# A ring of five tiles instead of four for gathered expert rows, in a streaming-encoder layer on one Trainium2 core

## The chip, the core and the metric

The kernel runs on one core of one Trainium2 chip. The metric is device time in microseconds (us) of one execution. A core has a matrix engine (TensorE; PE in the profile, its weight loads PEld), a vector engine (VectorE, DVE), a scalar engine (ScalarE, ACT), a general engine (GpSimd, POOL) and a queue engine (SyncE, SP). Each engine runs its own instructions in the order in which they stand in the program, and waits on semaphores for the others. DMA transfers are issued from SP, ACT and, where the rows to be read are chosen by an index, from POOL.

## What is computed

One layer of an encoder is applied to 1024 prompt tokens and 8 x 16 sample tokens, 1152 rows of 1024 floats, which the kernel treats as nine tiles of 128 tokens. The parts are two kinds of attention, a merge, and then a product-key retrieval of single-neuron experts (PEER):

```
q = (xi @ w_q).reshape(t, PEER_HEADS, 2, PEER_DK // 2)
s = jnp.einsum('thpc,hpnc->thpn', q, sub_keys).astype(jnp.float32)
top_s, top_i = lax.top_k(s, PEER_TOPK)
...
idx = jnp.take_along_axis(cand_i, pos, axis=-1)
g = jax.nn.softmax(best_s, axis=-1)
hid = jax.nn.gelu(jnp.einsum('thkd,td->thk', u[idx], xi).astype(jnp.float32))
wgt = (g * hid).astype(xi.dtype)
return jnp.einsum('thk,thkd->td', wgt, v[idx])
```

Each token chooses 8 heads x 16 = 128 of 16384 experts. An expert has one row of `u` and one of `v`, of 1024 floats each. A last step adds a gated per-layer embedding (PLE).

## The kernel before

The nine tiles are two groups: group 0 is tiles 8, 0, 1, 2 and group 1 is tiles 3 to 7. Both go through a norm, the attention units (`project`, `prompt`, `decode`), the merge (`merge_phase`) and the routing (`route_phase`, which finds the top 16 with `topk16`, L733 to L737, and makes the expert indices, L744 to L802).

The experts are then done in two ways.

- **Group 0 gathers.** For each of its four tiles POOL issues 128 indirect DMAs, each of which brings one `u` row per token (128 x 1024 floats, 512 KB), and DVE forms the dot product with the token's row in one instruction (L821, with a small read of the accumulator behind it). After a GELU and the gate, 128 indirect DMAs bring the `v` rows, and DVE adds each, weighted, into `gya` (L823). These are 1024 gathers (L818) and 1024 DVE steps of 128 x 1024. They are the steps of a generator, `gather_steps`, and every gathered tile comes from one ring:

```
r = gat.tile([P, D], F32, tag="ring", name=f"{'uv'[k // P]}{t}_{k % P}", bufs=RING)
nc.gpsimd.indirect_dma_start(out=r, out_offset=None, in_=I["pu" if k < P else "pv"],
                             in_offset=bass.IndirectOffsetOnAxis(ap=gi[:, kk:kk + 1], axis=0))
```

- **Group 1 is dense.** `hidden` computes all 16384 hidden values of its 640 tokens in 128 blocks `j` (L969, `hd`), `expand_phase` turns the routing into a dense weight matrix (L923 to L940, kept in DRAM as `G_d`), and `dense_phase` multiplies and sums: per block `j` DVE multiplies hidden values with weights (L998, `ge`), ACT and DVE split `ge`, `us` and `vs` in a high and a low part (L951, L952), and PE sums the products in groups of four blocks (L1020 to L1022, `py`), which DVE adds to `yacc` (L1023). Of the 128 blocks 36 (`PRE`) have their hidden values computed ahead, during the routing, with GpSimd forming the low parts.

Where the gathers stand is set in two places. `gathers(G0)` hands out 400 steps when group 0's routing is done, at the lowest priority, so they are spread over group 1's attention, merge and routing. `dense_phase` hands out `G1` = `G2` = 5 steps per block `j`, not ahead of that block's split (`issue_after`), until all 1024 are used. The rest is the scheduler's: it plays the program through a timeline of its own and puts, on each engine, what is ready and of highest priority next. Four tiles of 4 KB per partition form the ring, so gather number k can start once the DVE step of gather k - 4 has ended. POOL issues the gathers in order, among its other work (memsets L333, powers L215, low parts L198 and L952, products L929).

By the trace the execution falls in five stages. I name them for later use:

- **A** (0 to 860 us): group 0's attention, merge and routing; no gathers.
- **B** (860 to 1620): group 1's attention and merge, with gathers.
- **C1** (1620 to 1963): group 1's routing on DVE, with the last of the 400 gathers, and the ahead-of-time hidden values on PE.
- **C2** (1963 to 2206): `expand_phase`.
- **D** (2206 to 3830): `dense_phase`, with 624 gathers. PLE (161 us) ends the program.

Of the kernel before, what the change touches and what calls it, by code (L numbers as in the profile page):

```python
# [31 lines left out]
SETUP = -1500  # L32
SC = 3
NH = (6, 5)
RING = 4
GD = 2
SR = 2
UNITS = (4, 0, 1, 5, 2, 6, 3, 7)
# [8 lines left out]
def build(tc, I, O, dbg=None, stop=None):  # L47
# [758 lines left out]
    def gather_steps(tiles, res):  # L806

        for t in tiles:
# [6 lines left out]
            for k in range(2 * P):  # L815
                r = gat.tile([P, D], F32, tag="ring", name=f"{'uv'[k // P]}{t}_{k % P}", bufs=RING)
                kk = k % P
# [384 lines left out]
```

## Time and profile before

| | |
|---|---|
| median of 3 runs | 3990.67 us (3986.85 to 3994.92) |
| the profiled execution, its own time | 3992.47 us |
| its span, first to last instruction | 3990.7 us |
| busy: PE, DVE, POOL, ACT | 3611.7, 2952.4, 1862.6, 1477.4 us |
| mean granted TensorE clock | 0.962 of full speed |
| moved by DMA | 1002.51 MB, 251 GB/s over the span; by the gathers 536.94 MB |

The profile gives, for each group of like instructions, its busy time and the idle time of its engine just ahead of it, with what ended that idle time. A busy share is an average over stages; a stage is read by its own window. The chain of work that ended last is followed back from the last instruction, at each step to what released it. Matmuls overlap in the records, so a group's busy time is a union and the mean length of one is more than its share.

### The profile page before, as it was taken

Reading aid. Unit: us, or ns where it says so; the run is one execution under the profiler, and the core shown is the slowest. Engines: PE = TensorE matmul, PEld = TensorE weight load, DVE = VectorE, ACT = ScalarE, POOL = GpSimd, SP = SyncE. Lnnn points to the kernel's source line nnn. Section 1 sums busy time; section 2 is a strip of 40 time slices with the busy share of each in tenths; the row PEclk is TensorE's granted clock in tenths of the full one; section 3 lists DMA queues with packets and bytes.
Section 4 is the critical chain, followed back from the end, with each engine's and each line's share of the span. In section 5 each row is a group of like instructions: output and inputs, shape, how many; then the busy total and the mean of one; then the engine's idle time right before and its main releaser. Section 6 shows DMA issues by size and latency. Waiting matters only on the chain.

```text
span 3990.7 us, 57379 instructions
## 1 busy us (share of the span) xinstructions
PE 3611.7 (91%) x20520; PEld 2990.8 (75%) x20520; DVE 2952.4 (74%) x5610; ACT 1477.4 (37%) x3379; POOL 1862.6 (47%) x1436
## 2 busy tenths in 40 slices
PE   7999898768888897899887999999999999999989
PEld 6656566656665565888887888888888888888866
DVE  5222113999878777899888688887889888888862
ACT  6555413356666311324578322222222222222231
POOL 5112122157676555663465355555555555555510
PEclk9999999889999998999999999999999999999999
DMA  7888625148888888983254898998999988989842
GB/s 218 251 261 244 191 64 193 48 134 258 285 277 273 303 303 304 328 263 114 99 216 211 290 317 303 320 320 294 320 312 316 326 313 300 320 310 322 303 152 70
DMA packets 415118, 1002.51 MB, mean 251 GB/s; under 512 B 38816, under 2 KB 170352, under 8 KB 412400
## 3 DMA queue, kind: packets, MB, share of 16 engines
q0 software_dynamic: 147456, 536.94, 39.1%
q1 hardware_dynamic: 237568, 397.63, 30.4%
q10 hardware_dynamic: 29808, 64.28, 4.2%
q8 instruction: 162, 2.65, 0.3%
q14 instruction: 124, 1.02, 0.1%
HBM read 917.19 MB, written 81.50 MB: 250 GB/s over the span
## 4 chain that ended last, share of the span: by engine, by line
PE 25%; DVE 22%; issue 20%; DMA 19%; POOL 12%; ACT 1%; POOLq 0%; SPq 0%; ACTq 0%; DVEq 0%
DMA v<-in_pv,gi 9%; POOL u L818 6%; DMA u<-in_pu,gi 5%; POOL v L818 4%; DVE u L821 4%; DVE gya L823 3%; PE hd L969 2%; PE pg L938 2%; PE Sd L552 2%; POOL ga L929 2%; PE pu L643 1%; DMA vs<-in_pv 1%; PE z L207 1%; PE z L208 1%; PE py L1020 1%
## 5 line engine op out<-in xcount | busy, mean ns | idle before, releaser
L818 POOL DMA_INDIRECT v<-in_pv,gi x512 | 669.6, 1308 | 595.5 <-DVE gya L823 466.9
L818 POOL DMA_INDIRECT u<-in_pu,gi x512 | 675.8, 1320 | 499.1 <-DVE u L821 361.0
L821 DVE SCALAR_TENSOR_TENSOR u<-u,gn 128x1024 f32<-128x1024 f32 x512 | 642.2, 1262 | 175.1 <-DMA u<-in_pu,gi 172.1
L823 DVE SCALAR_TENSOR_TENSOR gya<-v,hid,gya 128x1024 f32<-128x1024 f32 x512 | 661.3, 1292 | 116.6 <-DMA v<-in_pv,gi 112.3
L1020 PE MATMUL py<-vh,wh 128*128 128x512 f32 x1280 | 509.6, 400 | 61.8 <-DVE yacc L1023 35.5
L1021 PE MATMUL py<-vl,wh 128*128 128x512 f32 x1280 | 503.2, 394 | 0.3 <-DVE vl L952 0.3
L1022 PE MATMUL py<-vh,wl 128*128 128x512 f32 x1280 | 498.6, 394 | 3.3 <-DVE wl L952 3.3
L969 PE MATMUL hd<-aTh,ul 128*128 128x320 f32 x2048 | 483.8, 314 | 12.5 <-POOL ul L952 10.5
L969 PE MATMUL hd<-aTh,uh 128*128 128x320 f32 x2048 | 486.1, 315 | 7.8 <-ACT gp L972 4.9
L969 PE MATMUL hd<-aTl,uh 128*128 128x320 f32 x2048 | 483.2, 313 | 0.0
L969 PEld LDWEIGHTS hd<-aTh,ul 128*128 128x128 f32 x2048 | 350.5, 191 | 20.3 <-POOL ul L952 13.5
L969 PEld LDWEIGHTS hd<-aTh,uh 128*128 128x128 f32 x2048 | 352.7, 191 | 15.9 <-ACT gp L972 5.7
L969 PEld LDWEIGHTS hd<-aTl,uh 128*128 128x128 f32 x2048 | 351.5, 191 | 4.7
L1020 PEld LDWEIGHTS py<-vh,wh 128*128 128x128 f32 x1280 | 243.4, 190 | 122.4 <-DVE yacc L1023 43.8
L951 ACT CAST vh<-vs 128x1024 fp32r<-128x1024 f32 x128 | 133.9, 1052 | 461.6 <-PE py L1022 235.1
L1022 PEld LDWEIGHTS py<-vh,wl 128*128 128x128 f32 x1280 | 243.5, 190 | 56.0 <-DVE wl L952 5.3
L1021 PEld LDWEIGHTS py<-vl,wh 128*128 128x128 f32 x1280 | 243.9, 191 | 47.7 <-DVE vl L952 0.6
L951 ACT CAST wh<-ge 128x640 fp32r<-128x640 f32 x128 | 91.8, 727 | 436.6 <-PE py L1021 233.3
L951 ACT CAST uh<-us 128x1024 fp32r<-128x1024 f32 x128 | 134.3, 1049 | 276.0 <-PE hd L969 253.9
L1023 DVE TENSOR_TENSOR yacc<-yacc,py 128x1024 f32<-128x1024 f32 x160 | 192.5, 1215 | 16.0 <-PE py L1022 14.2
L938 PE MATMUL pg<-obb,ga 128*128 128x128 f32 x1280 | 163.8, 281 | 36.0 <-POOL ga L929 15.9
L938 PEld LDWEIGHTS pg<-obb,ga 128*128 128x128 f32 x1280 | 153.0, 191 | 45.6 <-POOL ga L929 20.0
(1053 smaller groups left out, 7260.4 us busy)
## 6 DMA issues: line engine op xcount, KB each, us to landing
us<-in_uT SPq DMA_DIRECT2D x128, 512.0 KB
vs<-in_pv SPq DMA_DIRECT2D x128, 512.0 KB
G_d<-stage ACTq DMA_DIRECT2D x10, 4096.0 KB
gj<-G_d SPq DMA_DIRECT2D x64, 640.0 KB
kcd<-in_kA SPq DMA_DIRECT2D x128, 256.0 KB
vcd<-in_vA SPq DMA_DIRECT2D x128, 256.0 KB
ge_d<-gp ACTq DMA_DIRECT2D x36, 320.0 KB
ge<-ge_d SPq DMA_DIRECT2D x36, 320.0 KB
```

What stands on the lines that cost most here:

```text
L552: nc.tensor.matmul(ps[32 * b4:32 * b4 + 32, :], q3[:, 4 * s + b4, :], rhs, start=br == 1 and q < nch, stop=True)
L818: nc.gpsimd.indirect_dma_start(out=r, out_offset=None, in_=I["pu" if k < P else "pv"], in_offset=bass.IndirectOffsetOnAxis(ap=gi[:, kk:kk ...
L821: nc.vector.scalar_tensor_tensor(r, r, 1.0, n2, op0=OP.mult, op1=OP.mult, accum_out=hid[:, kk:kk + 1])
L823: nc.vector.scalar_tensor_tensor(ya, r, hid[:, kk:kk + 1], ya, op0=OP.mult, op1=OP.add)
L929: nc.gpsimd.tensor_tensor(ga[:, c, :], oa[:, b, :, :].rearrange("p i c -> p c i"), gT[:, c0 + 4 * b:c0 + 4 * b + 4].unsqueeze(2).broadcast ...
L938: nc.tensor.matmul(pg[:, c * P:(c + 1) * P], ga[:, b0 + c, :], ob[:, b0 + c, :], start=True, stop=True)
L951: nc.scalar.copy(out_h, src)
L969: nc.tensor.matmul(ps[sp][:, 0:Nw], a[:, k, :], b[:, k, sp * Nw:(sp + 1) * Nw], start=k == 0 and q == 0, stop=k == 7 and q == 2)
L1020: nc.tensor.matmul(py[:, c], wh[:, ns], vh[:, c], start=a, stop=False)
L1021: nc.tensor.matmul(py[:, c], wh[:, ns], vl[:, c], start=False, stop=False)
L1022: nc.tensor.matmul(py[:, c], wl[:, ns], vh[:, c], start=False, stop=z)
L1023: nc.vector.tensor_tensor(yacc[n], yacc[n], py, op=OP.add)
```

## The change

One constant is changed. It is used once, as the number of buffers of the tag `ring` (L817).

```
-RING = 4
+RING = 5
```

The ring takes 4 KB more per partition, and gather k can start once the DVE step of gather k - 5 has ended. No instruction is added or taken out. Since the scheduler works with the ring's releases, the order on every engine changes from the first gathers on.

On VectorE in stage B, at the gathers of the first tile, this is before. `u` with a number is a gathered tile and `gn` the tokens' rows; the other rows are attention and the routing of a later tile (`oh`, `mn`, `kq`, `sm`).

```order
L821 SCALAR_TENSOR_TENSOR u_28_7958,hid_7873<-u_28_7958,gn_7869 128x1024
L450 RECIPROCAL sm_10175<-sm_10175 128x1
L794 TENSOR_TENSOR oh_7732<-oh_7732 128x64x8
L821 SCALAR_TENSOR_TENSOR u_29_7961,hid_7873<-u_29_7961,gn_7869 128x1024
L794 TENSOR_TENSOR oh_7724<-oh_7724 128x64x4
L317 TENSOR_TENSOR kq_10226<-kq_10226,kq115r 128x256
L821 SCALAR_TENSOR_TENSOR u_30_7964,hid_7873<-u_30_7964,gn_7869 128x1024
L794 TENSOR_TENSOR oh_7732<-oh_7732 128x64x4
L481 TENSOR_REDUCE mn_10280<-N_10274 128x1
L794 TENSOR_TENSOR oh_7724<-oh_7724 128x64x2
L318 TENSOR_TENSOR kq_10226<-kq_10226,kn 128x128
```

At the same place, with the same `oh` and the next `kq` and `mn`, the changed kernel has this.

```order
L821 SCALAR_TENSOR_TENSOR u_37_7985,hid_7873<-u_37_7985,gn_7869 128x1024
L794 TENSOR_TENSOR oh_7724<-oh_7724 128x64x4
L481 TENSOR_REDUCE mn_10367<-N_10361 128x1
L794 TENSOR_TENSOR oh_7732<-oh_7732 128x64x4
L450 RECIPROCAL sm_10283<-sm_10283 128x1
L821 SCALAR_TENSOR_TENSOR u_38_7988,hid_7873<-u_38_7988,gn_7869 128x1024
L821 SCALAR_TENSOR_TENSOR u_39_7991,hid_7873<-u_39_7991,gn_7869 128x1024
L317 TENSOR_TENSOR kq_10337<-kq_10337,kq116r 128x256
L794 TENSOR_TENSOR oh_7724<-oh_7724 128x64x2
L481 TENSOR_REDUCE mn_10392<-N_10386 128x1
```

Gather 37 now stands where gather 29 stood: the gathers stand more densely among the attention's steps. By the last norm step of the merge (L673) 339 gathers have been used before the change and 359 after it.

On VectorE at the head of C1, where the routing's top-16 search begins, the rows before the change are these. `tops`, `topi` and `sc` are the search's values, indices and scores, and `wq..l` a low part of the query weights.

```order
L821 SCALAR_TENSOR_TENSOR u_91_8923,hid_8649<-u_91_8923,gn_8645 128x1024
L733 MAX tops_14975<-sc_15046 128x8 x2
L733 MAX tops_14976<-sc_15060 128x8 x2
L734 MAX_INDEX topi_14980<-tops_14975,sc_15046 128x8 x2
L734 MAX_INDEX topi_14981<-tops_14976,sc_15060 128x8 x2
L735 MATCH_REPLACE sc_15046<-tops_14975,sc_15046 128x128 x2
```

And in the changed kernel the search begins behind another gather.

```order
L821 SCALAR_TENSOR_TENSOR u_112_8986,hid_8649<-u_112_8986,gn_8645 128x1024
L706 TENSOR_TENSOR wq12l<-wq12s,wq12h 128x1024
L733 MAX tops_14975<-sc_15046 128x8 x2
L733 MAX tops_14976<-sc_15060 128x8 x2
L734 MAX_INDEX topi_14980<-tops_14975,sc_15046 128x8 x2
L734 MAX_INDEX topi_14981<-tops_14976,sc_15060 128x8 x2
L735 MATCH_REPLACE sc_15046<-tops_14975,sc_15046 128x128 x2
```

The first steps of the search stand behind `u_112` instead of `u_91`, so of the 400 gathers 21 fewer follow the search's beginning.

In stage D the number of gathers by each group of four blocks stays nearly the same (417, 434, 451, 472 used after the first four groups before, 417, 435, 452, 471 after), and only their places between the dense steps move. On VectorE, in one group of D, before:

```order
L1023 TENSOR_TENSOR yacc_20596<-yacc_20596,py_23011 128x1024
L823 SCALAR_TENSOR_TENSOR gya_8647<-v_115_22498,hid_8649,gya_8647 128x1024
L1023 TENSOR_TENSOR yacc_20597<-yacc_20597,py_23037 128x1024
L823 SCALAR_TENSOR_TENSOR gya_8647<-v_116_22573,hid_8649,gya_8647 128x1024
L823 SCALAR_TENSOR_TENSOR gya_8647<-v_117_22576,hid_8649,gya_8647 128x1024
L823 SCALAR_TENSOR_TENSOR gya_8647<-v_118_22579,hid_8649,gya_8647 128x1024
L823 SCALAR_TENSOR_TENSOR gya_8647<-v_119_22582,hid_8649,gya_8647 128x1024
L823 SCALAR_TENSOR_TENSOR gya_8647<-v_120_22585,hid_8649,gya_8647 128x1024
L1023 TENSOR_TENSOR yacc_20598<-yacc_20598,py_23063 128x1024
```

The same stretch in the changed kernel:

```order
L1023 TENSOR_TENSOR yacc_20596<-yacc_20596,py_23011 128x1024
L823 SCALAR_TENSOR_TENSOR gya_8647<-v_117_22576,hid_8649,gya_8647 128x1024
L1023 TENSOR_TENSOR yacc_20597<-yacc_20597,py_23037 128x1024
L823 SCALAR_TENSOR_TENSOR gya_8647<-v_118_22579,hid_8649,gya_8647 128x1024
L823 SCALAR_TENSOR_TENSOR gya_8647<-v_119_22582,hid_8649,gya_8647 128x1024
L823 SCALAR_TENSOR_TENSOR gya_8647<-v_120_22585,hid_8649,gya_8647 128x1024
L823 SCALAR_TENSOR_TENSOR gya_8647<-v_121_22788,hid_8649,gya_8647 128x1024
L823 SCALAR_TENSOR_TENSOR gya_8647<-v_122_22791,hid_8649,gya_8647 128x1024
L1023 TENSOR_TENSOR yacc_20598<-yacc_20598,py_23063 128x1024
```

The gathers run two further ahead of `yacc` here, and as many stand between two additions as before. On SP, the loads and stores around a gathered tile (L811, L813, L828) move a few places forward among the weight loads, with the gathers that they belong to.

## The prediction

> **What bounds the kernel now.** I read the page's chain of waits first, then the table of stages, then the groups of instructions and the waits of each stage, and last the timeline of a few microseconds.
>
> ```profile
> ## 4 chain that ended last, share of the span: by engine, by line
> PE 25%; DVE 22%; issue 20%; DMA 19%; POOL 12%; ACT 1%; POOLq 0%; SPq 0%; ACTq 0%; DVEq 0%
> DMA v<-in_pv,gi 9%; POOL u L818 6%; DMA u<-in_pu,gi 5%; POOL v L818 4%; DVE u L821 4%; DVE gya L823 3%; PE hd L969 2%; PE pg L938 2%; PE Sd L552 2%; POOL ga L929 2%; PE pu L643 1%; DMA vs<-in_pv 1%; PE z L207 1%; PE z L208 1%; PE py L1020 1%
> ```
>
> The gathers, with POOL's issue, the transfer and the DVE step, are 31% of the chain (9 + 6 + 5 + 4 + 4 + 3), although PE is the busiest engine. The stages B, C1, C2, D and the PLE, in this order:
>
> ```profile
> core 0: us, PE busy (x) PEld busy (x) DVE busy (x) ACT busy (x) POOL busy (x), PEclk, DMA share, GB/s
> 860.00:1620.00 760.00, 648.00 (x3431) 475.81 (x3431) 620.74 (x1095) 357.89 (x939) 487.75 (x413) 0.94 0.86 287
> 1620.00:1963.00 343.00, 307.61 (x1924) 296.85 (x1925) 331.13 (x1300) 118.71 (x197) 168.74 (x99) 0.94 0.60 199
> 1963.00:2206.00 243.00, 207.05 (x1597) 197.37 (x1598) 206.63 (x242) 192.02 (x507) 142.52 (x84) 0.99 0.46 187
> 2206.00:3830.00 1624.00, 1555.77 (x8241) 1379.68 (x8239) 1376.65 (x1517) 377.05 (x535) 846.98 (x621) 0.99 0.89 311
> 3830.00:3991.00 161.00, 148.22 (x576) 106.48 (x576) 59.21 (x80) 37.27 (x60) 4.41 (x8) 0.95 0.28 93
> ```
>
> B has no full engine: PE is idle for 112 us and DVE for 139. C1 is DVE's (331 of 343 us). D is nearly PE's (1556 of 1624), with DVE and the DMA engines (0.89) close behind. What leaves DVE idle in B are these groups:
>
> ```profile
> L821 DVE SCALAR_TENSOR_TENSOR u<-u,gn 128x1024 f32<-128x1024 f32 x211 | 261.5, 1245 | 76.2 <-DMA u<-in_pu,gi 73.8 <-issue 1.7 <-DVE sm L450 0.3
> L823 DVE SCALAR_TENSOR_TENSOR gya<-v,hid,gya 128x1024 f32<-128x1024 f32 x128 | 164.0, 1281 | 44.9 <-DMA v<-in_pv,gi 44.1
> ```
>
> 118 of the 139 idle us are DVE standing at a gathered row that has not landed (73.8 + 44.1). In D the same groups, with what PE waits for there:
>
> ```profile
> L823 DVE SCALAR_TENSOR_TENSOR gya<-v,hid,gya 128x1024 f32<-128x1024 f32 x368 | 472.2, 1283 | 71.8 <-DMA v<-in_pv,gi 68.2
> L821 DVE SCALAR_TENSOR_TENSOR u<-u,gn 128x1024 f32<-128x1024 f32 x256 | 310.0, 1221 | 96.1 <-DMA u<-in_pu,gi 95.5
> DVE u L821 <- DMA u<-in_pu,gi: 95.5, 72, 4.4
> DVE gya L823 <- DMA v<-in_pv,gi: 68.2, 67, 3.4
> PE py L1020 <- DVE yacc L1023: 35.5, 27, 3.7
> PE py L1020 <- ACT wh L951: 20.9, 14, 3.8
> PE py L1020 <- ACT vh L951: 5.4, 2, 5.1
> ```
>
> DVE loses 164 us to gathers in D, in 139 waits of 1.2 us on average. PE loses about 62 us there, 35.5 of it directly to additions of DVE that come late, and 20.9 to `wh`, which ACT makes from DVE's `ge`.
>
> **How long a gather takes.** The ring's turn shows in D, in DVE's rows and one of POOL's:
>
> ```profile
> 3007.79 1.28 DVE L823 SCALAR_TENSOR_TENSOR gya<-v,hid,gya 128x1024 f32<-128x1024 f32 x1
> 3009.72 1.28 DVE L823 SCALAR_TENSOR_TENSOR gya<-v,hid,gya 128x1024 f32<-128x1024 f32 x1
> ...
> 3018.60 1.28 DVE L823 SCALAR_TENSOR_TENSOR gya<-v,hid,gya 128x1024 f32<-128x1024 f32 x1 [0.86 <-DMA v<-in_pv,gi]
> ...
> 3011.27 0.93 POOL L818 DMA_INDIRECT v<-in_pv,gi  x1 [0.66 <-DVE gya L823]
> ```
>
> The step at 3009.72 ends at 3011.00 and frees its tile; POOL starts the gather at 3011.27; the step that uses it starts at 3018.60, after a wait. So from release to use a gather needs 7.6 us here, and with four tiles only the three steps between and whatever the program puts among them cover it. With five tiles this gather would be released by the step at 3007.79, which ends 1.93 us earlier. That is more than its wait of 0.86.
>
> **The change part by part.** Nothing is added or taken out, so each term is stall that goes, or work that moves.
>
> *D: stalls.* Each gather gets at least one more DVE step as cover, 1.22 to 1.28 us by the rows above, and on average the 2.5 us between two gathers of D (1624 us / 624). The average wait is 1.2 us, the longest 4.4. So most of the 139 waits go; I keep a quarter, 40 of 164 us, since the scheduler also moves steps. The numbers of gathers per group of blocks stay, so no DVE work moves into D. The end gains only what PE gains. Its floor comes from two stretches without waits:
>
> ```profile
> 3107.07 0.39 PE L1020 MATMUL py<-vh,wh 128*128 128x512 f32 x1
> ...
> 3113.19 0.39 PE L1020 MATMUL py<-vh,wh 128*128 128x512 f32 x1
> 3179.70 0.46 PE L969 MATMUL hd<-aTh,ul 128*128 128x320 f32 x2
> ...
> 3182.34 0.46 PE L969 MATMUL hd<-aTh,ul 128*128 128x320 f32 x2
> ```
>
> 27 `py` matmuls in 6.12 us are 0.227 us each, and 18 `hd` in 2.64 are 0.147. By the code the stage has 128 blocks x 30 (five tiles, two halves, three products) = 3840 of the first, and (128 - 36) blocks x 48 = 4416 of the second: 871 + 648 = 1519 us. So D cannot fall by more than 105 us, and of this only the 62 of waits belong to DVE or ACT. I take 40 of the 62: all but a few of the `yacc` waits and a part of the `wh` waits. The bounds are 0 (the transfers, already at 0.89, give nothing) and 62.
>
> *B: stalls against denser work.* The waits behind the 118 us:
>
> ```profile
> DVE u L821 <- DMA u<-in_pu,gi: 73.8, 72, 5.3
> DVE gya L823 <- DMA v<-in_pv,gi: 44.1, 50, 2.6
> DVE kq L317 <- POOL kq135r L215: 1.4, 1, 1.4
> ```
>
> They would fall to about 40 by the same reasoning (122 waits of 0.97 us on average; one step more is at least 1.2, but the scheduler here packs the steps more densely, which takes part of the cover back). Against it, 20 more gathers stand in B: 20 x (1.25 + 0.08 for the read of the accumulator) = 27 us of DVE work, the 0.08 from this row:
>
> ```profile
> L821 DVE DVE_READ_ACCUMULATOR u<-u,gn 128x1 f32 x210 | 17.0, 81 | 0.0
> ```
>
> DVE's clock in B thus gains 78 - 27 = 51 us. PE has 112 idle us there, but part of these are waits on ACT that no gather causes:
>
> ```profile
> PE mt13t L224 <- DVE tg L647: 17.4, 2, 16.5
> PE po L503 <- ACT pT L80: 15.2, 12, 4.4
> PE pt L496 <- ACT pT L80: 14.4, 12, 3.1
> PE pt L496 <- ACT p L451: 9.5, 3, 5.8
> ```
>
> The first is DVE late at the merge's end and can go whole; the `pT` waits stay. I take 30 us, between 0 and 51. One reason excludes less than nothing unless transfers slow down: the added 27 us are smaller than the stall that the ring's turn must lose.
>
> *C1: work that leaves.* The routing's search stands behind fewer gathers, and DVE is its bound. The prices there:
>
> ```profile
> L821 DVE SCALAR_TENSOR_TENSOR u<-u,gn 128x1024 f32<-128x1024 f32 x46 | 72.0, 1571 | 2.8 <-DMA u<-in_pu,gi 2.8
> L823 DVE SCALAR_TENSOR_TENSOR gya<-v,hid,gya 128x1024 f32<-128x1024 f32 x16 | 25.1, 1568 | 0.0
> ```
>
> A step takes 1.57 us in C1 and 1.25 in B. In C1, POOL forms the low parts for the hidden values at the same time. 20 steps that leave are worth 20 x 1.57 = 31 us; at B's price they would be 25. I take 28. C2 starts when the routing is done, so it moves forward whole; its own length stays (243 us, PE, DVE and POOL in turn).
>
> The Trainium skill, "SBUF — State Buffer", section "Who interferes with whom", says that a VectorE instruction with two SBUF inputs and a GpSimd instruction that reads SBUF lock each other out of a shared port for a whole instruction. By that rule the longer step is such a lock, and the term would be the 31; without it the 25. The 1.571 against 1.245 agrees in direction.
>
> *At no cost:* the 4 KB of memory; the loads of `gn` and `gya` that move forward on SP, by a few weight loads, and stay prefetches; POOL's small work in B (memsets, powers), queued behind gathers that now wait less. If that cover failed, the nearest price is the last row above, 1.4 us of DVE behind a power in all of B.
>
> *The sum.* -30 (B) -28 (C1) -40 (D) = -98 us. The profiled execution took 3992.47 us (span 3990.7), 1.8 above the median of 3990.67. 3992.5 - 98 = 3894.5; set against the median it is 3893. I give 3894.
>
> **The rivals.**
>
> 1. *Transfers or PE take D over.* DVE's stalls shrink, but D is at 0.89 of the DMA engines and PE at 96%, so D gains 5 us or none, and only B and C1 count, somewhat cut: -58 to -63, about 3932. For it: D moves 311 GB/s over 1624 us, and the best of the page's 40 slices is 328:
>
> ```profile
> GB/s 218 251 261 244 191 64 193 48 134 258 285 277 273 303 303 304 328 263 114 99 216 211 290 317 303 320 320 294 320 312 316 326 313 300 320 310 322 303 152 70
> ```
>
> At that rate D could fall to 1624 x 311 / 328 = 1540 at best. Against it: that still leaves 84 us, more than the 40. Chance 0.24.
>
> 2. *The change does nothing that counts.* The scheduler plans with the same fifth tile, so it sets the steps so much closer that the cover stays as it was. The order in B goes this way (gather 37 where 29 stood), but in D the count per group is unchanged. 3990, chance 0.06.
>
> 3. *A fifth gather in flight makes each slower.* With five tiles the ring turns as fast as before if the time from release to use grows by 5/4, from 7.6 to 9.5 us. Beyond that it is a loss. The place is B and D, where 122 + 139 waits show the ring as the limit. At 10.1 us each such step would come (10.1 / 5) - (7.6 / 4) = 0.12 us later than now, 31 us if all 261 stay ring-bound; and the 27 us that B takes on are not paid back by its stalls, but C1 returns its 28. So about +30, 4022. For it: DMA share 0.86 and 0.89 in the two stages. Against it: gathers are the same number and bytes, and more in flight adds no traffic. Chance 0.10.
>
> The Trainium skill, "DMA: Bandwidth & Descriptors", section "Queues, rings and completion order", says that a DMA engine takes turns between queues by whole packets, and drains a queue's ring in order. By that rule a fifth gather stands behind the other four of its queue and lands no sooner where the queue is never empty, which is rival 1 or 3. The queue rows speak against a full queue: the gathers' own packets take 39.1% of the engines' span.
>
> ```profile
> q0 software_dynamic: 147456, 536.94, 39.1%
> q1 hardware_dynamic: 237568, 397.63, 30.4%
> ```
>
> **How the numbers follow.** The forecast has 0.60: 3894, with its own range from all terms high (62 + 51 + 31 = 144, 3848) to half of each (3943). With the rivals' 0.24, 0.06 and 0.10 the chances sum to one. The range that should hold 8 in 10 runs from 3850 to 3985: it leaves out rival 3, rival 2 and the very best case. What a measurement of this kernel can tell from no change is about 0.2%, 8 us. Faster by more: forecast and rival 1, 0.84. Same: 0.06. Slower: 0.10.
>
> **What would show it.** In the profile after: DVE's idle time at L821 and L823 behind DMA falls from 118 to about 40 us in B and from 164 to about 40 in D; `PE py <- DVE yacc` falls from 35.5 below 15; B is about 730 us long, C1 about 315, D about 1584. C2 keeps its 243. The forecast is wrong if D stays above 1615 while DVE's stalls go (rival 1), if the stalls stay near 280 us in all (rival 2), or if the time from a release to its use rises over 9.5 us (rival 3).

## The result, and the profile after

| | before | after |
|---|---|---|
| median | 3992.8 us (3986.85 to 3999.76, 4 runs) | 3864.45 us (3856.23 to 3871.44, 4 runs) |
| profiled execution | 3992.47 us | 3856.23 us |
| mean granted TensorE clock | 0.962 | 0.968 |

The ratio is 0.968, with a 95% interval of 0.966 to 0.969: 128 us less by the medians, 136 by the two profiled executions. The forecast was 3894, its range 3850 to 3985.

The chain of waits of the changed kernel (shares of the span, by engine and by line) is now PE's:

```profile
PE 50%; DVE 20%; issue 11%; DMA 9%; POOL 7%; ACT 3%; SPq 0%; ACTq 0%; POOLq 0%; DVEq 0%
PE hd L969 11%; PE py L1022 5%; PE py L1020 5%; PE py L1021 5%; POOL v L818 3%; PE pu L643 3%; DVE u L821 2%; POOL u L818 2%; DMA u<-in_pu,gi 2%; PE Sd L552 2%; DVE gya L823 2%; PE zg L208 2%; PE zg L209 2%; PE zg L207 2%; PE pg L938 2%
```

The gathers' lines, 31% of the chain before, are 11% here (3 + 2 + 2 + 2 + 2); the transfers of `v`, 9% before, have dropped out of the list. The dense matmuls stand at its head. The table of stages of the changed kernel has the columns of the one before: window, length, busy time of PE, PEld, DVE, ACT and POOL, granted clock, DMA share, GB/s.

```profile
core 0: us, PE busy (x) PEld busy (x) DVE busy (x) ACT busy (x) POOL busy (x), PEclk, DMA share, GB/s
867.00:1597.00 730.00, 640.87 (x3401) 472.57 (x3399) 635.27 (x1112) 354.98 (x923) 529.41 (x432) 0.95 0.90 314
1597.00:1914.00 317.00, 283.31 (x1784) 274.45 (x1785) 294.89 (x1258) 114.18 (x189) 132.03 (x74) 0.94 0.52 174
1914.00:2155.00 241.00, 216.28 (x1718) 210.09 (x1717) 222.94 (x242) 197.42 (x515) 152.39 (x87) 1.00 0.49 198
2155.00:3696.00 1541.00, 1530.90 (x8261) 1371.37 (x8259) 1372.84 (x1517) 377.39 (x537) 874.59 (x620) 1.00 0.93 327
3696.00:3855.00 159.00, 144.34 (x576) 104.20 (x576) 58.66 (x80) 37.29 (x60) 5.35 (x8) 0.98 0.28 94
```

Against the rows before, B is 760 to 730, C1 343 to 317, C2 243 to 241, D 1624 to 1541, the PLE 161 to 159. D fell most, by 83 us, twice what was forecast for it. PE is now busy for 1530.90 of D's 1541 us.

DVE's waits in D, and below them PE's, with total, times and longest in us:

```profile
DVE yacc L1023 <- PE py L1022: 37.1, 25, 4.8
DVE u L821 <- DMA u<-in_pu,gi: 32.7, 25, 2.8
...
DVE gya L823 <- DMA v<-in_pv,gi: 16.3, 22, 1.4
...
PE py L1020 <- ACT wh L951: 4.9, 5, 2.9
PE py L1022 <- DVE wl L952: 1.8, 3, 1.2
...
PE py L1020 <- DVE yacc L1023: 0.4, 1, 0.4
```

DVE's stalls behind gathered rows fell from 164 to 49 us (32.7 + 16.3), and `yacc <- PE` (14.2 before, 37.1 now) has taken the first place in DVE's list. PE hardly waits for DVE any more. In B the same groups read:

```profile
DVE u L821 <- DMA u<-in_pu,gi: 41.0, 56, 2.7
DVE gya L823 <- DMA v<-in_pv,gi: 11.8, 21, 1.6
...
PE mt13t L224 <- DVE tg L647: 5.3, 1, 5.3
```

118 became 53 us, and PE's wait at the merge's end 17.4 became 5.3.

### The profile page after: what moved, and what is told of

Its sections match the earlier page's. It is cut to its first block, busy times and chain, and to the rows that moved or that the text cites. A ratio compares the mean times of both kernels' runs of the same rounds, so it can differ in the third digit from the quotient of the medians.

```text
span 3854.5 us, 57390 instructions
## 1 busy us (share of the span) xinstructions
PE 3571.1 (93%) x20520; PEld 2973.5 (77%) x20520; DVE 2949.6 (77%) x5610; ACT 1480.2 (38%) x3379; POOL 1911.3 (50%) x1436
## 4 chain that ended last, share of the span: by engine, by line
PE 50%; DVE 20%; issue 11%; DMA 9%; POOL 7%; ACT 3%; SPq 0%; ACTq 0%; POOLq 0%; DVEq 0%
PE hd L969 11%; PE py L1022 5%; PE py L1020 5%; PE py L1021 5%; POOL v L818 3%; PE pu L643 3%; DVE u L821 2%; POOL u L818 2%; DMA u<-in_pu,gi 2%; PE Sd L552 2%; DVE gya L823 2%; PE zg L208 2%; PE zg L209 2%; PE zg L207 2%; PE pg L938 2%
## 5 line engine op out<-in xcount | busy, mean ns | idle before, releaser
L818 POOL DMA_INDIRECT v<-in_pv,gi x512 | 697.6, 1362 | 488.6 <-DVE gya L823 368.8
L818 POOL DMA_INDIRECT u<-in_pu,gi x512 | 689.7, 1347 | 398.4 <-DVE u L821 264.4
L821 DVE SCALAR_TENSOR_TENSOR u<-u,gn 128x1024 f32<-128x1024 f32 x512 | 620.4, 1228 | 80.7 <-DMA u<-in_pu,gi 76.6
L1020 PE MATMUL py<-vh,wh 128*128 128x512 f32 x1280 | 498.2, 391 | 7.1 <-ACT wh L951 4.9
L1023 DVE TENSOR_TENSOR yacc<-yacc,py 128x1024 f32<-128x1024 f32 x160 | 193.4, 1214 | 40.7 <-PE py L1022 37.1
L938 PE MATMUL pg<-obb,ga 128*128 128x128 f32 x1280 | 157.1, 277 | 24.7 <-POOL ga L929 10.5
L929 POOL TENSOR_TENSOR ga<-oa,gT 128x512 f32<-128x512 bf16 x80 | 135.2, 1710 | 82.3 <-PE pg L938 67.3
```

The costliest lines, as they stand in the source:

```text
L821: nc.vector.scalar_tensor_tensor(r, r, 1.0, n2, op0=OP.mult, op1=OP.mult, accum_out=hid[:, kk:kk + 1])
L929: nc.gpsimd.tensor_tensor(ga[:, c, :], oa[:, b, :, :].rearrange("p i c -> p c i"), gT[:, c0 + 4 * b:c0 + 4 * b + 4].unsqueeze(2).broadcast ...
L938: nc.tensor.matmul(pg[:, c * P:(c + 1) * P], ga[:, b0 + c, :], ob[:, b0 + c, :], start=True, stop=True)
L1020: nc.tensor.matmul(py[:, c], wh[:, ns], vh[:, c], start=a, stop=False)
L1023: nc.vector.tensor_tensor(yacc[n], yacc[n], py, op=OP.add)
```

## The experiments

The theory after the result: each stage gains by itself what one more step of cover takes from its waits, so the parts add up; and the time grows again when a tile is taken away. The rivals: the gain of D is owed to what came ahead of it (the gathers' earlier start), or a gather that shares its queue with more others comes later, which a sixth tile would show. For all stage lengths of this section one set of marks is used: the first gather's DVE step, the last norm step (L673), the first `oa` (L923), the last `pg` (L938), the last `yacc` (L1023). By them the two kernels, and the runs below, read (us; no kernel leaves anything out of the computation; each ratio is to runs of before made on the same chip; stage A, not in the table, is 865 to 873 us, and 846 and 848 in the two runs of 3950.92 and 3966.76 us):

| | B | C1 | C2 | D | rest | median of runs | ratio to before (95%) |
|---|---|---|---|---|---|---|---|
| before, 4 tiles | 757 | 342 | 242 | 1625 | 160 | 3992.8 | 1 |
| after, 5 tiles | 730 | 318 | 241 | 1542 | 158 | 3864.45 | 0.968 (0.966 to 0.969) |
| 5 tiles, in D 4 | 731 | 318 | 241 | 1626 | 159 | 3949.81 | 0.990 (0.988 to 0.993) |
| 4 tiles, in D 5 | 758 | 341 | 241 | 1531 | 159 | 3905.59 | 0.979 (0.977 to 0.982) |
| 3 tiles | 802 | 393 | 230 | 1724 | 239 | 4255.19 | 1.066 (1.064 to 1.068) |
| 6 tiles, `kn` moved | 893 | 259 | 255 | 1539 | 159 | 3950.92 | 0.991 (0.988 to 0.994) |
| 5 tiles and a pad | 888 | 264 | 254 | 1547 | 160 | 3966.76 | 0.994 (0.992 to 0.995) |
| 6 tiles, `NH` (6, 4) | 748 | 290 | 248 | 1532 | 159 | 3845.29 | 0.963 (0.962 to 0.965) |
| 5 tiles, `NH` (6, 4) | 747 | 326 | 238 | 1540 | 159 | 3871.99 | 0.971 (0.968 to 0.973) |
| after, run again | 727 | 317 | 241 | 1539 | 160 | 3862.3 | 0.968 (0.966 to 0.969) |
| 6 tiles, fewer `qp` | 747 | 291 | 249 | 1533 | 159 | 3846.35 | 0.964 (0.961 to 0.967) |
| 6 tiles, fewer `lo` | 741 | 293 | 249 | 1532 | 159 | 3847.21 | 0.964 (0.961 to 0.967) |

### The fifth tile ahead of D alone

Only the first 400 gathers use five tiles; those of D use four.

```
-        for t in tiles:
+        for ti, t in enumerate(tiles):
...
-                r = gat.tile([P, D], F32, tag="ring", name=..., bufs=RING)
+                q = 2 * P * ti + k
+                r = gat.tile([P, D], F32, tag=f"ring{q % 5 if q < G0 else (q - G0) % 4}", name=..., bufs=1)
```

> Five tiles for the first 400 gathers (stages B and C1), four for the 624 of D. Theory (each stage is paid by its own ring's turn): B and C1 as in the changed kernel, 730 and 317 us, and D as before, 1624 us with 164 us of DVE at gathers that have not landed and PE waiting 35 us for yacc; about 3940 us, 52 less than before. Rival (the new order as a whole, not the ring's turn in D, made D shorter, for instance because D starts from a better state): D falls too, below 1580, and the time is near 3890.

Measured: 3949.81 us. B and C1 are those of the changed kernel (731, 318), D is that of before (1626).

### The fifth tile in D alone

The same edit with `q % 4 if q < G0 else (q - G0) % 5`.

> Four tiles for the first 400 gathers, five for the 624 of D. Theory: B and C1 as before, 757 and 342 us, D as in the changed kernel, 1541 us, with DVE's waits for gathers near 50 us and PE's waits near 10; about 3909 us, 84 less than before. Rival (new order as a whole): D keeps a good part of its 1624, and the time is above 3940.

Measured: 3905.59 us, B and C1 as before the change (758, 341), D 1531. Against the median of before beside them (3991.09 us, 7 runs) the two parts give 41.3 and 85.5 us, 127 together, and the whole change gave 128: they add up, and D's gain needs nothing from the stages ahead of it. Both kernels hold five tiles of memory throughout, so the 4 KB alone cost nothing here: B and C1 of the second are those of before. D of the two kernels, first the one with four tiles there, then the one with five:

```profile
2160.00:3786.00 1626.00, 1558.56 (x8251) 1380.72 (x8249) 1376.94 (x1518) 376.75 (x535) 838.68 (x621) 0.99 0.89 311
```

```profile
2212.00:3743.00 1531.00, 1523.60 (x8241) 1368.44 (x8239) 1374.63 (x1517) 375.58 (x535) 866.81 (x620) 1.00 0.93 329
```

DVE's work is equal (1377 and 1375 us), and its stalls behind gathered rows are 159 and 46 us. PE's idle time falls by 60 us (67.4 to 7.4), and its busy time, for the same matmuls, by 35. The prediction had no term for the second part. No run holds the order of the instructions as it was and changes the ring alone, so what the scheduler's own moves within D add to the effect is not told apart.

### Three tiles

```
-RING = 4
+RING = 3
```

> Three tiles throughout. Theory (release to use takes 7.5 us whatever the ring, so three tiles allow a gather every 2.5 us at best, which is just D's pace of 2.5): every unevenness stalls, DVE's waits for gathers in D rise from 164 to 400 us or more, D to about 1840 us; in B 313 gathers at 2.5 us make it some 800 us long, and C1 takes 26 more steps, about 40 us; in all near 4290 us. Rival (each tile is worth the same, about 130 us, as an effect of order): 4120 us.

Measured: 4255.19 us, a ratio of 1.066. The direction is as the theory has it, in every stage that holds gathers. D's part came otherwise than expected: it is 1724 us and not 1840, and the last gathers run past it into the PLE (239 instead of 160). The premise of 7.5 us whatever the ring does not hold: the steps of D that wait for a row stand 6.2 us (median) behind the release with three tiles, and 7.8 with four. From three to four tiles D and its tail give 178 us, from four to five 85. DVE's stalls in D with three tiles, for comparison:

```profile
DVE gya L823 <- DMA v<-in_pv,gi: 174.3, 155, 3.9
DVE u L821 <- DMA u<-in_pu,gi: 162.9, 115, 4.3
```

The sums of these two groups are 337, 164 and 49 us for three, four and five tiles: each tile takes away less.

### Six tiles

Six tiles need another 4 KB; `kn` (1 KB) was moved to the attention's pool to make room.

```
-RING = 4
+RING = 6
-    kn = const.tile([P, 2, P], F32, name="kn")
...
+    kn = act.tile([P, 2, P], F32, name="kn")
```

> Six tiles throughout; to make room, one small constant (kn, 1 KB) lies in a pool that is closed ahead of D. All 400 first gathers now stand ahead of the merge's last norm step, 41 more than with five tiles. Theory (D is at 1541 us against a floor of 1519 from undisturbed matmuls, and PE waits 10 us): D gains 10 us at most; C1 loses 41 steps of 1.57 us, 64 us, and B takes 41 of 1.33, 54 us of DVE, into idle time of which it has about 95, so it grows by some 15; about 3815 us. Rival (each tile is worth the same): 3735 us. Rival (B is full, and gives all of it back): 3860.

Measured: 3950.92 us, far off. C1 (259) and D (1539) are as the theory has them; B takes 893 instead of 730. The trace of that kernel shows one wait, in PE's list between 840 and 1760 us:

```profile
PE z L207 <- ACT vU L311: 184.9, 3, 182.8
```

and the table of 760 to 970 us, first of this kernel, then of the changed kernel with five tiles:

```profile
760.00:970.00 210.00, 20.58 (x85) 17.10 (x85) 200.35 (x803) 27.50 (x55) 109.55 (x90) 0.54 0.60 210
```

```profile
760.00:970.00 210.00, 159.10 (x848) 124.95 (x846) 204.75 (x837) 120.74 (x365) 121.10 (x99) 0.88 0.55 178
```

PE stands nearly still for 183 us: group 1's attention does not run beside group 0's routing any more. In ACT's order the last routing copy (`oh`, L788) of group 0 stands ahead of the first attention copy of group 1 (`kq`, L310) here, and that copy then waits another 22.7 us for DVE's `fl` (L306). In the changed kernel the first copy stands 445 rows of ACT's trace ahead of the last `oh` (and 444 with `kn` moved and five tiles, in the control with `NH` (6, 4) further down). Was that the sixth gather in flight, or the 4 KB?

### Five tiles and 4 KB that nothing uses

Five tiles, `kn` moved as above, and one further tile of 4 KB that is written once and never read.

```
+        pad = gat.tile([P, D], F32, name="pad")
+        nc.vector.memset(pad[:, 0:1], 0.0)
```

> Five tiles, and a sixth tile of 4 KB that is allocated beside them and never used (one element is set); kn lies as in the run with six tiles. Theory (with 4 KB more the first attention tiles of group 1 come to lie on memory of the routing of group 0, so the attention starts only when that routing is done): B is near 890 us and C1 near 260, as with six tiles, and the time near 3950 us. Rival (the sixth gather in flight is what made B slow): B is 730 us, C1 317, and the time 3864.

Measured: 3966.76 us, B 888, C1 264. The pad alone does it, by the same wait of PE:

```profile
966.82 0.70 PE L207 MATMUL z<-wu14h,aTh 128*128 128x392 f32 x1 [183.99 <-ACT vU L311]
```

So it is the memory that the sixth tile takes, not a sixth gather in flight. What in the placement of the tiles makes ACT's copies and DVE's `fl` stand so late was not traced further.

### Six tiles with room made elsewhere

The number of weight buffers `NH` goes from (6, 5) to (6, 4), `kn` is moved, and the ring is 6. The control has the same `NH` with five tiles.

```
-NH = (6, 5)
-RING = 4
+NH = (6, 4)
+RING = 6
```

> Six tiles, and one weight buffer pair less in the attention of group 1 (6 KB), so that the attention's tiles lie clear of the routing's again; kn moved as before. 376 gathers stand ahead of the merge's last norm step, 17 more than with five tiles. Theory: B is back near 735 us, C1 loses 17 x 1.57 = 27 us and is near 290, D is 1540, at its floor: 3840 us. Rival (a sixth tile is worth nothing more, B pays what C1 gains): 3864. Rival (sixth gather in flight makes B slow): B stays above 800 us, 3930 or more.

> Five tiles with the same smaller weight buffers and kn moved: the control for the run before. 357 gathers ahead of the merge's last norm step. If the weight buffers have slack, stages and time are those of the changed kernel, 3864 us; if not, B grows, and the run before has to be read against this one.

> The changed kernel again, on the same chip as the three runs above, to set them against: 3864 us, B 730, C1 317, C2 241, D 1541.

Measured: 3845.29 us with six tiles, 3871.99 for the control, 3862.3 for the changed kernel run again beside them. The missing weight buffer costs about 10 us by the medians, though the intervals of the two ratios touch (17 to 20 in B of the profiled executions; that of the control lies 11 us above its median). The sixth tile gives 27 against its control, and there the intervals are apart. That gain is in C1 (326 to 290), with 376 instead of 357 gathers used by the end of B; C2 gives 10 of it back (238 to 248). In D the sixth tile gives 8 us at most (1540 to 1532).

### Two other places for the room

One buffer less of the staging tile `qp` in group 1's projections (`nts` instead of `nts + 1`); and, apart from it, four buffers for the low parts of the `wu1` weights. Both with `kn` moved and six tiles.

> Six tiles; kn in the attention's pool; the room comes from one buffer less of the staging tile qp in group 1's projections, so that the attention of group 1 starts early again. Nothing is left out. Theory (what a sixth tile gives comes as one more step of cover, as in C1 and D of the run with six tiles and fewer NH buffers): B 735 to 750, C1 about 285, D 1530 to 1540, time 3825 to 3845. Rival (the buffer that is missing holds the projections, so that PE or ACT wait there and B pays for what C1 gains): B over 765, time 3860 or more.

> Six tiles; kn in the attention's pool; the room comes from fewer buffers (4) of the low parts of the weights wu1, those of group 1's unit projections. Nothing is left out. Theory: as with the smaller qp, B 735 to 750, C1 about 285, D 1530 to 1540, time 3825 to 3845. Rival: PE waits for low parts in B, B over 765, time 3860 or more.

Measured: 3846.35 and 3847.21 us, at or just past the upper end of what was expected. Neither is told apart from the kernel with fewer `NH` buffers (3845.29): each pays for its room with 10 to 20 us in B (747 and 741 against 727 to 730), as that one does (748). All three lie about 16 us below the changed kernel run again; for the one with fewer `NH` buffers, made beside it, the intervals of the ratios are apart (0.962 to 0.965 and 0.966 to 0.969). D of the kernel with fewer `qp`:

```profile
2152.00:3685.00 1533.00, 1526.49 (x8256) 1370.51 (x8254) 1376.51 (x1518) 375.26 (x536) 874.11 (x619) 1.00 0.93 329
```

PE is idle for 6.5 us of it, so more tiles can give D next to nothing.

## Why the prediction was right, and where it was not

**B, predicted 30, measured 27 to 30.** Of the 78 us of stall that were to go, 65 went (118 to 53). DVE's work grew by 15 us instead of 27 (620.74 to 635.27): the 20 gathers came, with some 22 us, but about 8 us of other DVE work left the stage. The two misses nearly cancel (51 against 50 us), and PE's idle time fell by 23 (112 to 89). The 30 itself was picked between 0 and 51, so that it fits this well is partly luck.

**C1, predicted 28, measured 24 to 26.** Close, by two errors of opposite sign, which is luck. DVE's groups of this stage in the changed kernel (count, then busy and mean ns):

```profile
L821 DVE SCALAR_TENSOR_TENSOR u<-u,gn 128x1024 f32<-128x1024 f32 x25 | 31.7, 1282 | 2.9 <-DMA u<-in_pu,gi 2.9
L823 DVE SCALAR_TENSOR_TENSOR gya<-v,hid,gya 128x1024 f32<-128x1024 f32 x16 | 26.5, 1657 | 0.0
```

21 `u` steps left (46 to 25), and with them 40 us (72.0 to 31.7), 1.92 each and not 1.57: more of the long ones went than of the short ones. All of DVE's busy time fell by 36 us (331.13 to 294.89). But its idle time rose from 12 to 22, with a wait that the move made:

```profile
DVE wq12l L706 <- ACT wq12h L705: 6.1, 1, 6.1
```

The rows of the changed order, shown with the change, have this `wq12l` just ahead of the search. The prediction priced the rows that left and not the row that then stood in front.

The two prices of a step, 1.57 in C1 and 1.25 in B, are told apart by what POOL does at the same time. Three long steps before the change, with one of the usual length ahead of them, and the POOL rows beside them:

```profile
1642.03 1.22 DVE L821 SCALAR_TENSOR_TENSOR u<-u,gn 128x1024 f32<-128x1024 f32 x1
1643.17 3.42 DVE L821 SCALAR_TENSOR_TENSOR u<-u,gn 128x1024 f32<-128x1024 f32 x1
1681.84 3.90 DVE L821 SCALAR_TENSOR_TENSOR u<-u,gn 128x1024 f32<-128x1024 f32 x1
1692.35 2.80 DVE L821 SCALAR_TENSOR_TENSOR u<-u,gn 128x1024 f32<-128x1024 f32 x1
...
1642.95 2.55 POOL L952 TENSOR_TENSOR ul<-us,uh 128x1024 fp32r<-128x1024 f32 x1
1682.24 2.41 POOL L952 TENSOR_TENSOR ul<-us,uh 128x1024 fp32r<-128x1024 f32 x1
1691.69 2.38 POOL L952 TENSOR_TENSOR ul<-us,uh 128x1024 fp32r<-128x1024 f32 x1
```

Each long step overlaps a low part on POOL, and is longer by 1.6 to 2.7 us, where the product takes 2.4 to 2.55. Counted over C1 before the change, the 15 steps that overlap such a POOL product take 2.66 us on average, the 46 others 1.22. How far they overlap matters: the 11 with 0.88 us or more take 1.96 to 4.07 us, and the four with 0.53 or less, the first row above among them, the usual 1.2. The Trainium skill, "SBUF — State Buffer", section "Who interferes with whom", gives the rule that the prediction weighed (an exclusive lock on a shared port); the traces agree with it. That rests on overlaps in the trace; no run here took POOL's products away.

**D, predicted 40 with bounds of 0 and 62, measured 83.** The mechanism was right (DVE's stalls fell to 49 us, where 40 were to stay, and PE's waits for `yacc` went from 35.5 to 0.4, below the 15 that were named), and the size was wrong in two ways. D lies outside its own bounds; the whole time fell inside the stated range because B gave 27 to 30 of the 51 that it was allowed. The first: "I take 40 of the 62: all but a few of the `yacc` waits and a part of the `wh` waits." Nearly all went. PE's idle time in D is length less busy time, 1624 - 1555.77 = 68 before and 1541 - 1530.90 = 10 after: 58 us. The `wh` waits on ACT (20.9 to 4.9) were DVE's too, since ACT makes `wh` from a `ge` that DVE's stalls had made late; in the two half changes they are 22.6 us and nothing. The second: the bound of 62 held only waits, but PE's busy time for the same matmuls fell as well, by 25 us. This is what stands behind a wait before the change, in PE's rows:

```profile
2997.42 0.39 PE L1021 MATMUL py<-vl,wh 128*128 128x512 f32 x1
3001.08 0.53 PE L1020 MATMUL py<-vh,wh 128*128 128x512 f32 x1 [3.27 <-ACT wh L951]
3001.42 0.62 PE L1021 MATMUL py<-vl,wh 128*128 128x512 f32 x1
3001.84 0.63 PE L1022 MATMUL py<-vh,wl 128*128 128x512 f32 x1
3002.26 0.63 PE L1020 MATMUL py<-vh,wh 128*128 128x512 f32 x1
...
3004.40 0.60 PE L1022 MATMUL py<-vh,wl 128*128 128x512 f32 x1
...
3005.30 0.40 PE L1022 MATMUL py<-vh,wl 128*128 128x512 f32 x1
3005.53 0.39 PE L1020 MATMUL py<-vh,wh 128*128 128x512 f32 x1
```

After a wait of 3.27 us the matmuls start 0.42 to 0.43 us apart for 3.4 us, and then again 0.23. The granted clock of these 3.4 us, in windows before, in and after the spell:

```profile
2994.50:2997.90 3.40, 3.31 (x15) 2.40 (x14) 1.92 (x2) 3.00 (x5) 0.00 (x0) 1.00 0.69 281
2997.90:3001.30 3.40, 0.22 (x1) 0.22 (x2) 3.40 (x5) 1.57 (x3) 1.67 (x1) 1.00 0.66 223
3001.30:3004.70 3.40, 3.40 (x9) 2.67 (x9) 3.40 (x4) 1.95 (x4) 1.09 (x1) 0.52 0.93 329
3004.70:3008.10 3.40, 3.40 (x16) 2.77 (x16) 3.40 (x5) 0.42 (x2) 2.74 (x2) 0.98 1.03 336
```

Half the clock, after one such stretch without work. The spells add up to 41.0 us in D before and 6.8 after; at half the rate a spell loses half its length, so at most 20.5 - 3.4 = 17 of the 25 us are this. The other 8 stand mostly at the edges of the waits: PE's work in D is in 56 pieces before and in 14 after, and the last `py` of a piece counts 0.39 us as busy where it would be followed after 0.23, which is some 42 x 0.16 = 7 us. The two half changes agree: 41.0 us of half clock in D with four tiles there, 3.4 with five; with three tiles it is 100. The Trainium skill, "TensorE: Matmul & The Clock Gate", section "Part 1: The HAM clock gate (the "warmup" mystery)", states a half-rate clock after an idle window of about 3.4 us, and full rate after as long a busy one. The traces agree on the half rate and the 3.4 us; but of the waits of PE at whose end the 11 spells of D stand before the change, 7 are shorter than 3.4 us, the shortest 1.76.

The records show more. The 11 spells begin whole multiples of 3.413 us apart (the first two 218.45 us, 64 of them). With D cut into windows of that length on the same grid, the 11 windows just ahead of a spell hold 1.76 to 3.41 us without PE work, and no window that full clock followed holds more than 1.86. In the changed kernel the two ahead of a spell hold 1.65 and 1.79, the others at most 1.56. So in these traces a window idle for about half its length was enough.

The floor of 1519 us for D held: 1542, and 1531 to 1533 in the best runs.

**Time from release to use.** The prediction had it at 7.6 us with four tiles. In the changed kernel, a step in D that waits for its row, the step five gathers earlier, and the POOL row that the latter released:

```profile
3116.73 1.22 DVE L821 SCALAR_TENSOR_TENSOR u<-u,gn 128x1024 f32<-128x1024 f32 x1
...
3125.61 1.23 DVE L821 SCALAR_TENSOR_TENSOR u<-u,gn 128x1024 f32<-128x1024 f32 x1 [1.21 <-DMA u<-in_pu,gi]
...
3118.22 1.28 POOL L818 DMA_INDIRECT u<-in_pu,gi  x1 [2.77 <-DVE u L821]
```

The first step ends at 3117.95, and the row is used at 3125.61 when it lands: 7.7 us. That is one gather against one. Over all gathers of D, the time from POOL's issue to the last packet has a median of 5.94 us after and 5.85 before: the transfer itself, from first packet to last, takes 2.39 instead of 2.50, and the time from the end of the issue to the first packet 2.25 instead of 2.02. **Rival 3** needed a growth by 5/4, and its loss did not come; the runs with six tiles say the same (6.0 to 6.1 us, with a D no longer than with five).

**Rival 1** (D at its transfers' limit, 3932) fell as well: D moves 327 GB/s with a share of 0.93. That is close to the 328 on which its floor of 1540 was reckoned. Five tiles in D alone went below that floor, to 1531 us at 329 GB/s, with PE busy for 1523.60; so the best slice of before was no limit, and PE is the engine that bounds D now. The prediction weighed a rule of the Trainium skill here, "DMA: Bandwidth & Descriptors", section "Queues, rings and completion order": a DMA engine drains a queue's ring in order. By this a fifth gather would stand behind the other four and land no sooner; that did not decide, for the gather above took 7.7 us and not 9.5. The 39.1% that was set against a full queue is a mean over the span; within D the gathers' own packets take 56.9% of the engines before and 58.3% after, so it was weaker evidence than it looked. **Rival 2** (nothing) fell in every stage that holds gathers.

**C2** kept its length, as predicted, and moved forward.

The sum was -98, and the profiled executions differ by 136. By the marks of the table D gave 43 more than its term, C2 and the rest 3, B and C1 together 7 less, and A 1 less. One figure of the working was slightly off: 1624 us for 624 gathers is 2.6 us a gather and not 2.5.

## What to carry to other kernels

A ring's wait is priced by comparing the time from release to use (7.6 us in one row here, a median of 7.8 over the waits of D) with the steps that cover it; here the covering step was about as long as the mean wait (1.2 us each), and each further tile took away less stall in D (337, 164, 49 us with three, four and five). Where such waits reach TensorE, count what follows them too: here 58 us of idle time took 25 of busy time with them, at most 17 of it half clock. And a tile costs its memory: 4 KB that nothing used cost this kernel about 100 us, so a longer ring is tried together with the place from which its room is taken.

## What was not expected of the hardware

- The half clock comes behind waits that are quite short. D has 11 spells of it before the change, one of 6.8 us and the others of 3.4; at the start of each, or a few us ahead, stands a wait of PE of 1.76 to 5.1 us. The length of a wait alone does not decide: four others of 2.25 to 2.32 us brought no spell.
- A DVE step of 128 x 1024 with two operands in SBUF took up to 3.9 us in the rows above instead of 1.22, beside a POOL product of 2.4 us; the mean of 1.57 in C1 is a mixture of two kinds of step, not a price of its own.
- A fifth tile hardly slowed the single gather: from issue to last packet 5.94 us in D instead of 5.85, at DMA shares of 0.93 and 0.89. From three tiles to four it had grown by more, from 5.31.
